# A hybrid encoder layer on one core: two chunk chains started together, and the second pair's transposes among the last chunks

## The chip, the cores and the metric

The kernel runs on 1 core of one Trainium2 chip. The metric is the device time of one execution in microseconds, as the median of several runs. The engines are TensorE (PE; its weight loads are PEld), VectorE (DVE), ScalarE (ACT) and GpSimd (POOL), and SyncE (SP), which issues most transfers.

## The reference

Two sequences (`x_prompt`, `x_sample`) of 1024 rows and 1024 columns go through the same layer. All numbers are float32.

```
h   = rmsnorm(x, g_mix) * (1 + sc1) + sh1
z   = h @ w_in                      # q_lat, kv_lat, k_pe, f_in
mix = concat(mla(q_lat, kv_lat, k_pe), fourier(f_in)) @ w_out
x   = x + ga1 * mix
h2  = rmsnorm(x, g_ffn) * (1 + sc2) + sh2
x   = x + ga2 * ((silu(h2 @ w_gate) * (h2 @ w_up)) @ w_down)
y   = rmsnorm(x, g_final)
```

The vectors `sh1`, `sc1`, `ga1`, `sh2`, `sc2`, `ga2` are slices of `silu(c) @ w_ada + b_ada`, one set for each sequence. Only `h` and `z` of the first rows, and the weights that are prepared for them, concern this change.

## The kernel before

A float32 product is made of three matmuls of two rounded parts each (`mm3`, lines 79 to 81): high by high, high by low, low by high. `split` (63, 64) makes the parts: a cast on ACT and a subtraction on DVE.

The first stage makes z and the Fourier input of all rows. Rows are taken in eight pairs of 128 (`pairs`; four for each sequence): the two halves u = 0, 1 of a pair are turned into their sum ("even") and difference ("odd"), and both are multiplied by the input weights: `z_mm` by `wz` (448 columns), `f_mm` by `wcs` (280 or 256 columns), in eight steps c of 128 channels each. Pairs 2 to 7 load x already transposed (`xt_load`), scale it by the row norms, which PE spreads with two transposes (`scale_t`, 450), and make even and odd on POOL (`evenodd`, 497).

Pairs 0 and 1 run while weights still arrive. Their x is loaded in rows, `norm` (425) takes squares on ACT (423), a root on POOL (`rstd`, 104 to 111), scales the rows (435, 436) and makes sum and difference (441, 150, 153); `flip` (464) transposes two channel blocks of both by PE (475), and ACT and DVE apply scale and shift and split the result (478 to 485).

The scale `s1` and shift `sh1` that `flip` needs come from the first 2048 columns of `w_ada`. They are made in four **chunks** g of 2 MB, each for two channel blocks: `cols_load` (248) fetches it, `cols_mm` (256) multiplies it by silu(c) into a row, `cols_vecs` copies the row to `modrow` on ACT (261), turns it with four small matmuls (264), and DVE writes `s1`, `sh1` (271 to 275). Then `flip(0, g)`, `z_part(g)` and `f_part(g)` (12 matmul rows each) follow for pair 0. Beside this run `prep` (392 to 402: the Fourier weights from `w_in`), `wz_split` (387), and `fold_out` (310, 311: `w_uv` of each of four heads multiplied into `w_out`, with a store to `wo_d`).

`first_pair` then evacuates pair 0 (`z_finish`, 529 to 537), transposes pair 1's rows (`flip(1, g)`), and transposes pair 0's latents (`latents`, 580). `pair(k)` does the rest, with `between` as a hook in the middle of z. The generator `extras`, advanced by `next(more)`, loads eight tiles of further `w_ada` columns (231) and multiplies them (241), one "conditioning group" of eight matmuls for each.

Order: each engine runs its own queue in order. `then` and `behind` (`tc.issue_after`) put a function behind the last matmul, cast or subtraction written; within these bounds the order on an engine is set when the program is built, and a tile's new owner waits for its last user. SP issues loads and stores in the order of its queue, so a load that waits for a tile holds all that is behind it. Tiles matter in three places: `xtile` (four of 4 KB), `wada_tile` (two slots of 8 KB) and the `wide` tiles `hh0`, `hh1`, `hl0`, `hl1`, used in turn for weights, chunks, output weights and later x. PSUM has eight banks.

## Time and profile before

| | us |
|---|---|
| times of three runs | 2021.83, 2017.2, 2017.96 (median 2017.96) |
| the profiled execution: time | 2021.76 |
| its span | 2020.0 |
| PE busy in the span | 1979.0 (98%) |
| DVE busy | 1389.5 (69%) |
| ACT busy | 897.1 (44%) |
| POOL busy | 844.1 (42%) |

The span is what the trace covers; all places below are in us from its start. "Busy" is the union of an engine's instructions; matmuls overlap, so a row's second number (its own duration) is more than the distance to the next row, and only distances between starts tell the rate. `[1.20 <-ACT eoh L481]` in a row is idle time before it and what ended it. An "x8" joins consecutive instructions. The granted clock is TensorE's, 1.00 at full speed.

### The profile page before, as it was taken

To read this page: it belongs to the slowest core of one execution; us is meant where nothing else is said; L and a number is where in the kernel's file an instruction comes from. 1 tells how busy PE (TensorE), PEld (TensorE's weight loads), DVE (VectorE), ACT (ScalarE), POOL (GpSimd) and SP (SyncE) were. 2 spreads that over 40 slices of the span, in tenths; PEclk is the share of its full clock that TensorE was granted. 3 is DMA by queue.
4 is the path that set the end of the run, shared out by engine and by line. 5 is a ranking of instruction groups with operands and counts; after the bars stand their busy time and mean duration, and the time that the engine had idled before them with its cause. 6 is when DMAs were issued, how large, how long until landed. Compare 5 with 4: busy or idle time off the path is not lost.

```text
span 2020.0 us, 27660 instructions
## 1 busy us (share of the span) xinstructions
PE 1979.0 (98%) x9554; PEld 1622.5 (80%) x9554; DVE 1389.5 (69%) x2083; ACT 897.1 (44%) x1750; POOL 844.1 (42%) x1000
## 2 busy tenths in 40 slices
PE   7899999999999999999999999999999999999998
PEld 5688778888888877888888878887888888888886
DVE  4467757766687778677777567788755655656794
ACT  4665535555565564333333356443333333335551
POOL 0364312111223237878879410344654454420152
PEclk8899999999999999999999999999999999999999
DMA  8886984445543575555545586665333233257762
GB/s 348 292 297 202 306 325 118 120 98 123 148 117 108 184 262 200 194 170 199 194 159 196 172 311 231 220 224 190 122 105 105 99 110 105 99 192 248 250 229 88
DMA packets 179593, 376.59 MB, mean 186 GB/s; under 512 B 18012, under 2 KB 57564, under 8 KB 175740
## 3 DMA queue, kind: packets, MB, share of 16 engines
q1 hardware_dynamic: 157052, 305.60, 45.2%
q0 software_dynamic: 21824, 68.17, 11.0%
q8 instruction: 75, 1.23, 0.2%
q10 hardware_dynamic: 576, 1.05, 0.1%
q14 instruction: 66, 0.54, 0.1%
HBM read 262.75 MB, written 120.39 MB: 190 GB/s over the span
## 4 chain that ended last, share of the span: by engine, by line
PE 54%; DVE 4%; issue 2%; DMA 1%; POOL 1%; ACT 0%; SPq 0%; DVEq 0%; POOLq 0%; ACTq 0%
PE bank L80 18%; PE bank L79 18%; PE bank L81 18%; DVE wl L64 2%; DMA draw<-s_d 1%; DVE val L153 0%; DVE val L1873 0%; DMA val<-x_d 0%; DVE H L64 0%; DVE val L1901 0%; DVE val L1792 0%; ACT wh L63 0%; POOL rs_y L107 0%; POOL val L153 0%; DVE val L150 0%
## 5 line engine op out<-in xcount | busy, mean ns | idle before, releaser
L79 PE MATMUL bank<-H,wh 128*128 128x512 f32 x1232 | 480.5, 390 | 3.5 <-DVE val L153 1.4
L80 PE MATMUL bank<-H,wh 128*128 128x512 f32 x1232 | 479.5, 389 | 0.3 <-DVE H L64 0.3
L81 PE MATMUL bank<-H,wl 128*128 128x512 f32 x1232 | 479.3, 389 | 0.2 <-DVE wl L64 0.2
L79 PEld LDWEIGHTS bank<-H,wh 128*128 128x128 f32 x1232 | 231.3, 188 | 55.2 <-DVE val L1775 3.2
L64 DVE TENSOR_TENSOR wl<-draw,wh 128x512 fp32r<-128x512 f32 x286 | 210.1, 773 | 93.9 <-ACT wh L63 93.3
L81 PEld LDWEIGHTS bank<-H,wl 128*128 128x128 f32 x1232 | 231.3, 188 | 48.8 <-DVE wl L64 0.5
L80 PEld LDWEIGHTS bank<-H,wh 128*128 128x128 f32 x1232 | 231.3, 188 | 48.0 <-DVE H L64 0.6
L153 DVE TENSOR_TENSOR val<-bank,val 128x512 f32<-128x512 f32 x200 | 136.6, 689 | 161.3 <-PE bank L81 160.4
L63 ACT CAST wh<-draw 128x512 fp32r<-128x512 f32 x286 | 164.9, 619 | 175.5 <-PE bank L80 145.3
L153 POOL TENSOR_TENSOR val<-val 128x512 f32<-128x512 f32 x58 | 82.1, 1417 | 347.2 <-DVE val L1873 163.8
L80 PE MATMUL bank<-wl,wh 128*128 128x512 f32 x572 | 223.5, 391 | 1.8 <-DVE wl L64 1.7
L79 PE MATMUL bank<-wh 128*128 128x512 f32 x572 | 222.8, 390 | 1.2 <-ACT wh L63 1.1
L81 PE MATMUL bank<-wh,wl 128*128 128x512 f32 x572 | 222.6, 389 | 0.0
L63 ACT CAST wh<-rgu 128x512 fp32r<-128x512 f32 x172 | 107.1, 623 | 258.6 <-PE bank L80 202.3
L63 ACT CAST wh<-val 128x512 fp32r<-128x512 f32 x133 | 82.3, 622 | 261.3 <-PE bank L80 242.4
L64 DVE TENSOR_TENSOR wl<-val,wh 128x512 fp32r<-128x512 f32 x133 | 129.7, 977 | 66.2 <-ACT wh L63 66.1
L64 DVE TENSOR_TENSOR wl<-rgu,wh 128x512 fp32r<-128x512 f32 x172 | 160.0, 930 | 1.6 <-ACT wh L63 1.6
L150 POOL TENSOR_TENSOR val<-rgu 128x512 f32<-128x512 f32 x80 | 108.1, 1351 | 79.0 <-DMA rgu<-in_wgu_dram 75.2
L80 PEld LDWEIGHTS bank<-wl,wh 128*128 128x128 f32 x572 | 107.4, 188 | 26.9 <-DVE wl L64 4.7
L79 PEld LDWEIGHTS bank<-wh 128*128 128x128 f32 x572 | 107.4, 188 | 24.5 <-ACT wh L63 2.0
L81 PEld LDWEIGHTS bank<-wh,wl 128*128 128x128 f32 x572 | 107.4, 188 | 21.8
L150 POOL TENSOR_TENSOR val<-val 128x512 f32<-128x512 f32 x89 | 119.1, 1356 | 1.3
(398 smaller groups left out, 3917.2 us busy)
## 6 DMA issues: line engine op xcount, KB each, us to landing
rgu<-in_wgu_dram SPq DMA_DIRECT2D x86, 512.0 KB, 3.9
draw<-s_d SPq DMA_DIRECT2D x143, 256.0 KB, 3.3
s_d<-val POOLq DMA_DIRECT2D x88, 256.0 KB, 3.0
draw<-t_d SPq DMA_DIRECT2D x88, 256.0 KB, 4.2
s_d<-val SPq DMA_DIRECT2D x66, 256.0 KB, 3.8
draw<-in_w_down_dram SPq DMA_DIRECT2D x55, 256.0 KB, 4.2
xt<-in_x_dram SPq DMA_DIRECT2D x16, 512.0 KB, 8.3
wada<-in_w_ada_dram SPq DMA_DIRECT2D x16, 512.0 KB, 6.4
```

The lines of the kernel that those rows point to most:

```text
L63: here["a"] = nc.scalar.copy(hi, src).ins
L64: here["v"] = (eng or nc.vector).tensor_tensor(out=lo, in0=src, in1=rd(hi), op=ALU.subtract).ins
L79: nc.tensor.matmul(out, lh, rh, start=first, stop=False, skip_group_check=cont)
L80: nc.tensor.matmul(out, lh, rl, start=False, stop=False, skip_group_check=cont)
L81: here["t"] = here["pe"] = nc.tensor.matmul(out, ll, rh, start=False, stop=last, skip_group_check=cont).ins
L150: return eng.tensor_tensor(out=out, in0=x, in1=y, op=ALU.subtract).ins
L153: eng.tensor_tensor(out=out, in0=x, in1=y, op=ALU.add)
```

## The change

- The transfers on SP get another order. Chunk 0 and the second pair of Fourier weights go ahead of `wz`; chunks 1 to 3 go ahead of the output weights (`wo_load`), and chunk 2 now lies in the `wada` slots, chunk 3 in `hl0` and `hh0`, output weights 0 in a `wada` slot. `x_load(1)` stands ahead of chunk 3; `xt_load(2)`, `x_load(2)` follow the output weights.
- `cols_mm(1)`, `cols_vecs(1)` and `flip(0, 1)` stand ahead of `z_part(0)`, and likewise each following chunk one step earlier, so that the chain of one chunk runs beside the products of the one before.
- `norm(1)` comes beside chunk 3 (its sum goes to the `lq` tile), `flip(1, 0)` to `flip(1, 3)` between `z_part` and `f_part` 2 and 3, the folded heads between them; `norm(2)` starts in `first_pair`.
- The heads are folded in place (`fold_head`) and stored together (`fold_store`).
- Pair 0's latents and two steps of `more` move from `first_pair` to the first hook in pair 1's z.
- The even rows of pairs 0 and 1 share a tile (`st1["even"]`), and the second half of the subtraction goes from POOL to DVE.

The core of the diff:

```diff
@@ -434,11 +434,11 @@
                 return
             nc.scalar.activation(xt[0], xt[0], AF.Copy, scale=r[:, 0:1])
             nc.vector.tensor_scalar(out=xt[1], in0=xt[1], scalar1=r[:, 1:2], scalar2=None, op0=ALU.mult)
-            xe = w.tile([P, D], F32, tag="eo", name="xe", bufs=1)
+            xe = lq[0].rearrange("p a b -> p (a b)") if k else w.tile([P, D], F32, tag="eo", name="xe", bufs=1)
             for g in range(2):
                 gs = slice(512 * g, 512 * g + 512)
                 add(xe[:, gs], xt[0][:, gs], xt[1][:, gs], nc.vector)
-                sub(xt[0][:, gs], xt[0][:, gs], xt[1][:, gs], nc.gpsimd if g else nc.vector)
+                sub(xt[0][:, gs], xt[0][:, gs], xt[1][:, gs], nc.vector)
             st1["rows", k] = xe, xt[0]
 
         def scale_t(k):
@@ -464,9 +464,10 @@
         def flip(k, g):
             s, j = pairs[k]
             if g == 0:
-                st1["hf", k] = w3.tile([P, NC, 2, P], F32, tag="hf", name="hf", bufs=1)
+                if k == 0:
+                    st1["even"] = w3.tile([P, 2, NC, P], F32, tag="hf", name="hf", bufs=1)
                 st1["eo", k] = eo_tiles(k)
-            hf = st1["hf", k]
+            hf = st1["even"][:, k]
             (eh, el), (oh, ol) = st1["eo", k]
             pt = bank().rearrange("p (c u t) -> p c u t", c=2, u=2)
             for c in range(2):
@@ -475,14 +476,14 @@
                     here["pe"] = nc.tensor.transpose(pt[:, c, u, :], st1["rows", k][u][:, cc * P : (cc + 1) * P], ident).ins
             for c in range(2):
                 cc = 2 * g + c
-                nc.scalar.activation(hf[:, cc, 0], pt[:, c, 0], AF.Identity, bias=dsh[:, cc : cc + 1], scale=s1[s][:, cc : cc + 1])
+                nc.scalar.activation(hf[:, cc], pt[:, c, 0], AF.Identity, bias=dsh[:, cc : cc + 1], scale=s1[s][:, cc : cc + 1])
             for c in range(2):
                 cc = 2 * g + c
                 here["o"] = nc.scalar.activation(oh[:, cc], pt[:, c, 1], AF.Copy, scale=s1[s][:, cc : cc + 1]).ins
                 nc.vector.scalar_tensor_tensor(out=ol[:, cc], in0=pt[:, c, 1], scalar=s1[s][:, cc : cc + 1],
                                                in1=rd(oh[:, cc]), op0=ALU.mult, op1=ALU.subtract)
             gs = slice(2 * g, 2 * g + 2)
-            split(eh[:, gs], el[:, gs], hf[:, gs, 0, :])
+            split(eh[:, gs], el[:, gs], hf[:, gs])
 
         def evenodd(k):
 
@@ -575,7 +576,7 @@
             ti = 4 * u + j
             sk = st1.pop(("sk", k, u))
             pl = bank()
-            with tc.issue_after(here["t"]) if k > 0 else ExitStack():
+            with tc.issue_after(here["t"]):
                 for c in range(4):
                     nc.tensor.transpose(pl[:, c * P : (c + 1) * P], sk[:, c * P : (c + 1) * P], ident)
             if k + 1 < nk:
@@ -666,96 +667,95 @@
                 for c in range(2 * g, 2 * g + 2):
                     f_mm(0, pc[i], i, c)
 
-        def fold_heads(h, wo, outs):
-            then(fold_out, h, wo, wuvT, outs)
+        def fold_head(h):
+            t = (wo0, wo1)[h // 2]
+            then(fold_out, h, t, wuvT, [t[:, h % 2, 512 * g : 512 * g + 512] for g in range(2)])
+
+        def fold_store():
+            for dst, t in folded:
+                nc.sync.dma_start(dst, t)
+            folded.clear()
 
         wf_pair(0, "hh0")
         fold_q(wukT)
-        prep(0)
+        ring = [xtile() for _ in range(2)]
         x_load(0)
+        wt.append([cols_load(0, i, wada_tile()) for i in range(2)])
+        prep(0, 1, 2, 3)
+        norm(0)
+        wf_pair(2, "hl0")
         wz0 = wz_load(0, wide("hh1", (P, 4 * 512)))
-        wt.append([cols_load(0, i, wada_tile()) for i in range(2)])
-        prep(1)
-        norm(0)
-        prep(2, 3)
-        wf_pair(2, "hl0")
-        wt.append([cols_load(1, 0, *(xtile().rearrange("p (c n) -> p c n", n=512) for _ in range(2))), cols_load(1, 1, wide("hh0"))])
-        wz1 = wz_load(4, wide("hl1", (P, 4 * 512)))
-        wt.append([cols_load(2, i, wide(f"h{'hl'[i]}{1 - i}")) for i in range(2)])
-        pz, pc = ([bank() for _ in range(2)] for _ in range(2))
-        then(cols_mm, 0, wt[0])
-        wz_split(0, wz0)
-        prep(4, 5)
-        then(cols_vecs, 0)
-        then(flip, 0, 0)
+        wt.append([cols_load(1, 0, *(t.rearrange("p (c n) -> p c n", n=512) for t in ring)), cols_load(1, 1, wide("hh0"))])
         wuvT = w.tile([P, HEADS, KVL], F32, tag="gah1", name="wuvT")
         nc.sync.dma_start(wuvT, a["wuvT"])
         wpe = lq[1][:, 0].rearrange("p (a b) -> p a b", a=2)
         nc.sync.dma_start(wpe, a["wpe"])
+        wz1 = wz_load(4, wide("hl1", (P, 4 * 512)))
+        wt.append([cols_load(2, i, wada_tile()) for i in range(2)])
+        pz, pc = ([bank() for _ in range(2)] for _ in range(2))
+        then(cols_mm, 0, wt[0])
+        prep(4, 5)
+        then(cols_vecs, 0)
+        then(flip, 0, 0)
+        wz_split(0, wz0)
         prep(6, 7)
+        then(cols_mm, 1, wt[1])
+        x_load(1)
+        wt.append([cols_load(3, i, wide(f"h{'lh'[i]}0")) for i in range(2)])
+        then(cols_vecs, 1)
+        then(flip, 0, 1)
         wz_split(2, wz0)
         then(z_part, 0)
-        then(cols_mm, 1, wt[1])
-        wo0 = wo_load(0, wide("hl1", (P, 2, D)))
-        wt.append([cols_load(3, i, wada_tile()) for i in range(2)])
-        x_load(1)
+        then(cols_mm, 2, wt[2])
+        wo0 = wo_load(0, wada_tile().rearrange("p a b -> p (a b)").rearrange("p (a b) -> p a b", a=2))
+        fold_pe(wpe)
         then(f_part, 0)
-        then(cols_vecs, 1)
-        then(flip, 0, 1)
-        for i in (4, 6):
-            wz_split(i, wz1)
+        then(cols_vecs, 2)
+        then(flip, 0, 2)
+        wz_split(4, wz1)
         then(z_part, 1)
-        then(cols_mm, 2, wt[2])
+        then(cols_mm, 3, wt[3])
         wo1 = wo_load(1, wide("hl0", (P, 2, D)))
+        wz_split(6, wz1)
+        norm(1)
+        then(f_part, 1)
+        then(cols_vecs, 3)
+        then(flip, 0, 3)
+        then(z_part, 2)
+        xt_load(2)
         nc.sync.dma_start(ropec, a["ropec"])
         nc.sync.dma_start(ropes, a["ropes"])
-        then(f_part, 1)
-        then(cols_vecs, 2)
-        then(flip, 0, 2)
-        fold_pe(wpe)
-        fold_heads(0, wo0, (w.tile([P, 512], F32, tag="gah0", name="so"), lq[0][:, 0]))
-        then(z_part, 2)
-        then(cols_mm, 3, wt[3])
+        x_load(2)
+        then(flip, 1, 0)
         then(f_part, 2)
-        then(cols_vecs, 3)
-        then(flip, 0, 3)
-        fold_heads(1, wo0, [lq[g][:, 1] for g in range(2)])
-        with behind(), tc.issue_after(here["o"]):
-            norm(1)
-        for dst, so in folded:
-            nc.sync.dma_start(dst, so)
-        folded.clear()
+        then(flip, 1, 1)
+        fold_head(0)
+        then(z_part, 3)
+        then(flip, 1, 2)
+        fold_head(1)
+        then(f_part, 3)
+        then(flip, 1, 3)
+        more = extras()
+        next(more)
         nc.sync.dma_start(wq_d, wq)
         nc.sync.dma_start(sc_d, scT)
         nc.sync.dma_start(cmask, a["cmask"])
-        x_load(2)
-        more = extras()
-        next(more)
-        then(z_part, 3)
-        then(f_part, 3)
+        x_load(3)
+        fold_store()
         for h in (2, 3):
-            fold_heads(h, wo1, [wo1[:, h % 2, 512 * g : 512 * g + 512] for g in range(2)])
+            fold_head(h)
         wf.clear()
         lq.clear()
 
         def first_pair():
             z = z_finish(0, pz)
             next(z)
-            for g in range(4):
-                flip(1, g)
+            norm(2)
             next(more, None)
             next(z, None)
             for i in range(2):
                 f_finish(0, i, pc[i])
-            for u in range(2):
-                latents(0, u)
-            next(more, None)
-            next(more, None)
-            xt_load(2)
-            x_load(3)
-            for dst, so in folded:
-                nc.sync.dma_start(dst, so)
-            norm(2)
+            fold_store()
 
         def late_latents(k):
             if k > 0:
@@ -784,6 +784,11 @@
                     prepare(k + 1)
                     if k < 2:
                         norm(k + 2)
+                if c == 1 and k == 1:
+                    for u in range(2):
+                        latents(0, u)
+                    next(more, None)
+                    next(more, None)
                 if c == 1:
                     flush()
                 else:
```

What the order on the engines becomes. First PE, at the first z of pair 0: L392 is `prep`, L256 `cols_mm`, L264 `cols_vecs`, L475/L476 the transposes of `flip`, L79 to L81 with `wz` the z product. Before:

```order
L392 MATMUL bank_353<-c2_136,wide_269 128x128 x4
L392 MATMUL bank_364<-c2_136,wide_269 128x128 x4
L79 MATMUL bank_284<-wz_h_130,eoh_333 128x448
L80 MATMUL bank_284<-wz_l_131,eoh_333 128x448
L79 MATMUL bank_285<-wz_h_130,eoh_335 128x448
```

and now:

```order
L392 MATMUL bank_353<-c2_136,wide_269 128x128 x4
L392 MATMUL bank_364<-c2_136,wide_269 128x128 x4
L256 MATMUL bank_375<-xt_194,scT_141 32x512 x2
L256 MATMUL bank_375<-xt_193,scT_141 32x512 x2
L256 MATMUL bank_375<-wide_276,scT_141 32x512 x4
L264 MATMUL bank_394<-wq_129,modrow_392 128x2 x4
L476 MATMUL bank_403<-ident_67,xe_264 128x128
L476 MATMUL bank_403<-ident_67,xt_195 128x128
L476 MATMUL bank_403<-ident_67,xe_264 128x128
L476 MATMUL bank_403<-ident_67,xt_195 128x128
L79 MATMUL bank_287<-wz_h_130,eoh_334 128x448
L80 MATMUL bank_287<-wz_l_131,eoh_334 128x448
```

Chunk 1's matmuls, small matmuls and transposes moved ahead of the first z matmul; the small matmuls read `modrow`, which ACT has to write first.

Next PE in pair 1's z, at the transposes of `scale_t` (L450); L241 is a conditioning group. Before:

```order
L450 MATMUL bank_849<-ident_67,rs_r_810 128x128 x2
L79 MATMUL bank_824<-wz_h_130,eoh_676 128x448
L80 MATMUL bank_824<-wz_l_131,eoh_676 128x448
L241 MATMUL bank_787<-wada_784,scT_141 32x512 x4
L81 MATMUL bank_824<-wz_h_130,eol_677 128x448
L79 MATMUL bank_824<-wz_h_130,eoh_676 128x448
```

and now:

```order
L450 MATMUL bank_846<-ident_67,rs_r_741 128x128 x2
L79 MATMUL bank_795<-wz_h_130,eoh_583 128x448
L80 MATMUL bank_795<-wz_l_131,eoh_583 128x448
L81 MATMUL bank_795<-wz_h_130,eol_584 128x448
L79 MATMUL bank_795<-wz_h_130,eoh_583 128x448
L80 MATMUL bank_795<-wz_l_131,eoh_583 128x448
```

The second conditioning group went from here to pair 2's z, 108 rows later. Groups two to five now stand in pair 2: between them 11 z rows, then the latents and 10 f rows, then 17 f rows.

Last ACT, at the end of pair 0: L311 is a folded half head, L529/L530 and L542 to L544 `z_finish` with its squares, L478/L479 and L481/L482 the casts of `flip`. Before (`flip` of pair 1 follows behind):

```order
L529 ACTIVATE lat_655<-bank_284 128x448
L423 ACTIVATE junk_584,ms_581<-xt_405 128x1024
L610 COPY zc0_108<-bank_286 128x280
L542 ACTIVATE junk_659,mz_653<-lat_654 128x256
L543 ACTIVATE junk_659,mz_653<-lat_654 128x128
L435 ACTIVATE xt_404<-xt_404,rs_r_589 128x1024
L311 ACTIVATE wide_469<-bank_641,pk_140 128x512
L311 ACTIVATE wide_469<-bank_644,pk_140 128x512
L311 ACTIVATE wide_469<-bank_647,pk_140 128x512
L542 ACTIVATE junk_662,mz_653<-lat_655 128x256
L311 ACTIVATE wide_469<-bank_650,pk_140 128x512
L543 ACTIVATE junk_662,mz_653<-lat_655 128x128
```

and now:

```order
L611 COPY zc0_108<-bank_289 128x280
L543 ACTIVATE junk_720,mz_711<-lat_713 128x256
L479 ACTIVATE hf_333<-bank_672,wq_129,s1_77 128x128 x2
L482 ACTIVATE eoh_583<-bank_672,s1_77 128x128
L63 CAST eoh_583<-hf_333 128x256
L311 ACTIVATE wide_502<-bank_699,pk_140 128x512
L482 ACTIVATE eoh_583<-bank_672,s1_77 128x128
L311 ACTIVATE wide_502<-bank_702,pk_140 128x512
L311 ACTIVATE wide_502<-bank_705,pk_140 128x512
L311 ACTIVATE wide_502<-bank_708,pk_140 128x512
L544 ACTIVATE junk_720,mz_711<-lat_713 128x128
L611 COPY zs0_110<-bank_290 128x256
```

The last square of pair 0 (L543, now L544) stood behind four folded half heads and ahead of pair 1's casts; now it stands behind the same four and also behind the casts of all four flips of pair 1.

## The prediction

> **What bounds the kernel now.** I read the profile from whole to part: first the stretches of 20 us, then who TensorE (PE) waited for, then the timelines of the engines in the first 100 us. The stretches (columns: PE, weight loads, DVE, ACT, POOL busy, granted clock, DMA share, GB/s):
>
> ```profile
> 40.00:60.00 20.00, 20.00 (x123) 13.87 (x116) 4.96 (x22) 11.13 (x28) 1.15 (x3) 1.00 0.94 370
> 60.00:80.00 20.00, 14.92 (x66) 9.24 (x64) 11.23 (x32) 14.72 (x39) 8.66 (x20) 0.83 0.55 178
> 80.00:100.00 20.00, 15.71 (x88) 13.04 (x87) 7.82 (x19) 10.37 (x28) 7.54 (x8) 0.83 1.04 390
> 100.00:120.00 20.00, 20.00 (x130) 15.92 (x129) 10.61 (x23) 13.46 (x34) 12.70 (x25) 1.00 0.68 244
> ```
>
> From 40 to 60 and from 100 on PE is busy throughout; the lack is between: 5.1 us idle in 60 to 80 and 4.3 in 80 to 100, at a clock of 0.83. That is the place of this change. Everything behind 100 us has the same work in the same order but for the conditioning matmuls and a few stores, so a gain here is carried to the end. The waits of PE in the first 110 us:
>
> ```profile
> PE bank L241 <- DMA wada<-in_w_ada_dram: 4.3, 1, 4.3
> PE bank L450 <- POOL rs_r L111: 1.8, 1, 1.8
> PE bank L580 <- DVE lat L556: 1.7, 1, 1.7
> PE bank L79 <- ACT eoh L481: 1.2, 1, 1.2
> PE bank L475 <- DVE xt L150: 1.1, 1, 1.1
> ```
>
> Together 10.1 us. A wait costs more than itself: the matmuls behind it run slowly. After the 1.2 us wait for `eoh`:
>
> ```profile
> 35.12 0.74 PE L79 MATMUL bank<-wz_h,eoh 128*128 128x448 f32 x1 [1.20 <-ACT eoh L481]
> 38.58 0.37 PE L79 MATMUL bank<-wz_h,eoh 128*128 128x448 f32 x1
> ```
>
> Between these starts lie nine matmuls in 3.46 us, 0.38 each, against 0.20 later: about 1.5 us lost behind a wait of 1.2.
>
> **What the pieces cost.** The last chunk's rows on PE show each piece by the start of the next:
>
> ```profile
> 48.34 1.92 PE L256 MATMUL bank<-wada,scT 128*32 128x512 f32 x16
> 50.19 0.40 PE L79 MATMUL bank<-wcs_h,eoh 128*128 128x280 f32 x1
> 51.78 0.95 PE L264 MATMUL bank<-wq,modrow 128*128 128x2 f32 x8
> 52.58 0.30 PE L475 MATMUL bank<-ident,xe 128*128 128x128 f32 x1
> 53.05 1.88 PE L310 MATMUL bank<-wide,wuvT 128*128 128x512 f32 x4
> 54.70 0.47 PE L79 MATMUL bank<-wz_h,eoh 128*128 128x448 f32 x1
> 57.30 0.29 PE L79 MATMUL bank<-wcs_h,eoh 128*128 128x280 f32 x1
> 58.78 3.60 PE L310 MATMUL bank<-wide,wuvT 128*128 128x512 f32 x8
> 68.42 2.14 PE L580 MATMUL bank<-ident,lat 128*128 128x128 f32 x8 [1.66 <-DVE lat L556]
> 70.50 1.94 PE L241 MATMUL bank<-wada,scT 128*32 128x512 f32 x8
> 72.36 0.58 PE L79 MATMUL bank<-wz_h,eoh 128*128 128x448 f32 x1
> 92.51 0.29 PE L79 MATMUL bank<-wcs_h,eoh 128*128 128x280 f32 x1
> 98.44 0.36 PE L79 MATMUL bank<-wz_h,eoh 128*128 128x448 f32 x1
> ```
>
> Chunk matmuls 1.85, `f_part` 1.6, `cols_vecs` 0.8, `flip` 0.47, one folded head 1.65, `z_part` 2.6. Heads 2 and 3 took 3.6. The latents' eight transposes took 2.08 (four transposes of a `flip` took 0.47, so 0.94 would do: half clock again), one conditioning matmul group (L241) 1.86, pair 1's f 5.93 and its z (48 rows at 0.205) 9.8.
>
> The point to which I compare is pair 2's first z matmul, 98.44. The order moves the second conditioning group (1.86 us of work) from ahead of this point to behind it, so the old mark to be beaten is 96.6.
>
> **Start: chunk 1's row ahead of the first z.** Rows:
>
> ```profile
> 18.18 1.94 PE L256 MATMUL bank<-wada,scT 128*32 128x512 f32 x8 [0.47 <-DMA wada<-in_wada_dram]
> 20.04 2.70 PE L392 MATMUL bank<-c,wide 128*128 128x128 f32 x16
> 24.89 0.81 ACT L478 ACTIVATE hf<-bank,wq,s 128x128 f32<-128x128 f32 x2
> 28.62 0.18 ACT L401 CAST wcs_h<-bank 128x24 fp32r<-128x24 f32 x1 [0.35 <-DVE wcs_l L397]
> 20.87 1.07 DVE L64 TENSOR_TENSOR wz_l<-wide,wz_h 128x896 fp32r<-128x896 f32 x1
> GB/s 77 371 417 432 432 429 404 402 415 424 414 382 50 6 316 435 416 410 357 333 244 326 320 403 117 6 0 118 275 334 414 393 397 418 356 401 404 30 0 141
> ```
>
> The last row holds 40 slices of 2.75 us. `wz0` (128 x 1792 floats, 0.92 MB) now stands behind chunk 0 and the second weight pair. At about 430 GB/s these land 2.1 us earlier: chunk 0's second half starts at 16.05 instead of 18.18, and with its 1.94 the weight pair's matmuls start at 18.0 instead of 20.04. So `hf(0,0)` on ACT goes from 24.89 to 22.9.
>
> Chunk 1 has the same 9.2 MB ahead of its end as before. The slices add up to this at 24.7 us, and half a chunk's matmuls (0.9) end at 25.7. Then PE stands before `cols_vecs` 1, which needs a copy of chunk 1's row (modrow) on ACT. Before, `z_part` 0 filled this time. ACT has, from `hf` to its last weight cast, 3.9 us of work in the old rows (24.89 to 28.8). New in this stretch are the two casts of `wz_h`, each with a DVE partner of 1.07 us, for which the small casts at the end wait: 2.1. So 22.9 + 3.9 + 2.1 = 28.9, and the copy of 0.6 makes 29.5: **`cols_vecs` 1 starts at V = 29.7**, after a wait of 4.0. No row shows this wait; its bounds are 0.8 (the copy alone: V = 26.5) and 5.3 (V = 31, if the alternating ACT and DVE casts hide nothing of one another). I take 4.0, since it is put together from durations of the same instructions. Half clock behind it is charged with the 1.5 above.
>
> **From V to the folds.** In PE's order, us behind V: `flip(0,1)` ends at 1.3; `z_part` 0 with 1.5 for the clock 5.4; chunk 2 7.2; `f_part` 0 8.8; `cols_vecs` 2 and `flip(0,2)` 10.1; `z_part` 1 12.7; chunk 3 14.5; `f_part` 1 16.1. The transfers are in time: chunk 2 ends 12.8 MB, by the slices 33.3 us, needed at V + 5.4 = 35.1; chunk 3 ends 15.9 MB, 41 us at 410 GB/s, needed at 42.4. Before, the slices of 50 and 6 GB/s show the queue standing still at 33 to 38, behind the output weights; these now stand behind.
>
> Then ACT again. `norm(1)` now runs here, and row 3's copy stands behind its last step L435:
>
> ```profile
> 53.29 0.81 ACT L478 ACTIVATE hf<-bank,wq,s 128x128 f32<-128x128 f32 x2 [2.38 <-PE bank L475]
> 57.40 1.09 ACT L423 ACTIVATE junk<-xt 128x1024 bf16<-128x1024 f32 x1
> 58.35 0.24 ACT L423 ACTIVATION_READ_ACCUMULATOR junk<-xt 128x1 f32 x1
> 60.85 1.15 ACT L435 ACTIVATE xt<-xt,rs_r 128x1024 f32<-128x1024 f32 x1 [1.29 <-POOL rs_r L111]
> ```
>
> `hf` follows the start of `cols_vecs` by 1.5 (51.78 to 53.29), so it is at V + 10.3. Then one flip's first three casts, 1.3, and one square with its read, 1.2, end at 12.8; from the end of the read to L435 passed 2.3 (58.59 to 60.85) by way of POOL, so L435 runs from 15.0 to 16.1, the copy to 16.6. `cols_vecs` 3 starts at 16.7, a wait of 0.6 (bounds 0 and 1.9). `flip(0,3)` ends at 18.0, `z_part` 2 at 20.6. This short wait, with the nearly empty `cols_vecs` and `flip` behind it, resembles the 1.2 us one, so I charge its 1.5 again: 22.1. The Trainium skill, "TensorE: Matmul & The Clock Gate", section "Why this matters for your kernels", says that only idle gaps above about 3 us send the clock to half; the row at 35.12 contradicts it with 1.2 us. By the page this 1.5 would be left out and the time be 2008.5.
>
> Next: `flip(1,0)`, `f_part` 2, `flip(1,1)`, head 0, `z_part` 3: 0.47 + 1.6 + 0.47 + 1.65 + 2.6 = 6.8, to 28.9. `flip(1,2)`, head 1, `f_part` 3, `flip(1,3)`, heads 2 and 3: 0.47 + 1.65 + 1.6 + 0.47 + 3.6 = 7.8, to 36.7. Here z of pair 1 starts, at once: the old wait for `xt` (1.1) and the first part of that for `lat` are gone, since transposes and latents now have work beside them.
>
> **The latents.** They stand behind eleven z matmuls (2.3), at V + 39.0, and need `z_finish` of pair 0. ACT's rows:
>
> ```profile
> 61.91 1.82 ACT L311 ACTIVATE wide<-bank,pk 128x512 f32<-128x512 f32 x3
> 64.78 0.21 ACT L543 ACTIVATION_READ_ACCUMULATOR junk<-lat 128x1 f32 x1
> 69.63 0.41 ACT L63 CAST eoh<-hf 128x256 fp32r<-128x256 f32 x1
> 71.12 0.44 ACT L63 CAST eoh<-hf 128x256 fp32r<-128x256 f32 x1
> ```
>
> A flip's casts take 1.5 on ACT when nothing delays them (69.63 to 71.12), a folded half head 0.6. ACT from `z_part` 3's end at 28.9: copy of `lat` 0.4, `flip(1,2)` and head 1 2.7, squares and a copy 1.5, `flip(1,3)` and heads 2 and 3 3.9, together 8.5, so 37.4. PE's last fold at 36.7 and its cast set the same time, 37.3. Last square 0.5: 37.9. Then as before from the square's read (ending 64.99) to the latents at 68.42: 3.4, to 41.3. So **the wait for `lat` stays, at 2.3** (bounds 0 and 4), with the slow transposes of the 2.08.
>
> From 41.3: latents 2.1, conditioning group 1.9, thirteen z matmuls 2.7, transposes of `rs_r` 0.3, 24 z matmuls 4.9, f 5.9: 59.1. With V = 29.7, 88.8 against 96.6: **7.8 us gained**. The 4.3 us wait for `w_ada` and the 1.8 for `rs_r` are gone in this: that load's matmuls now stand behind pair 1's f, and pair 2's squares come while heads are folded.
>
> **What is moved beside this.** *Loads.* `x_load(1)`, `xt_load(2)` and `x_load(2)` are issued earlier on SP, all ahead of the folds; the old row shows what that saves, DVE standing before `scale_t`'s product:
>
> ```profile
> 87.13 2.48 DVE L453 TENSOR_TENSOR xT<-xT,bank 128x512 f32<-128x512 f32 x4 [9.91 <-DMA xT<-in_xt_dram]
> ```
>
> I count nothing for it, since PE's wait for `w_ada` covered it; without the move it would be late next, at 84 or so. `wuvT` and `wpe` (0.5 MB) now go ahead of `wz1`, which costs chunk 2 the 1.2 us that are in its 12.8 MB. *Stores.* The folded heads are written in place and stored later: the tile of heads 0 and 1 is a `wada` slot, freed by its stores behind `x_load(3)`; the tile of heads 2 and 3 is freed by stores that SP issues behind pair 0's `ckv_d`, hence near V + 44, and `xt_load(3)` waits for them. It is needed in the middle of pair 2's z, V + 64, 20 us later; nothing up to 4 us if SP is held up. *Even and odd rows of pair 2.* From `scale_t` to pair 2's z there are 24 z rows and f, 10.8 us. Before, the same chain had its product at 87.13 and its z at 98.44, 11.3 us, without a listed wait: tight, counted as nothing, bounds 0 and 1. *The subtraction* of the second half goes from POOL to DVE: nothing, since other casts stand beside it; at most the 1.1 us that PE waited for `xt`.
>
> The profiled execution took 2021.76 (span 2020.0), the median is 2017.96; two of the four times lie near 2021.8. 2021.76 - 7.8 = 2014.0, and from the median **2010**. I take the latter, since the new time will be a median too.
>
> **Rivals.** *ACT is the bound in both places.* For: ACT was busy 14.7 us of the 20 in 60 to 80 already, and its pieces now fall into less time. If durations add without overlap, V is 31.0, the latents wait 4.0, `cols_vecs` 3 waits 1.9: 4.3 us more, a gain of 3.5: 2014.5. Against: back to back the rows overlap.
>
> *No wait remains.* V = 26.5, no wait at the other two places and no half clock behind them: 3.2 + 0.6 + 2.3 + 1.5 + 1.5 + 1.1, 10 more: 2000. Against: each of the three waits is a chain of rows that the order only moves.
>
> *The change only moves the wait for `w_ada`.* Four conditioning groups (two loads each) now stand close together in pair 2, and the load of the third needs the slot of the first:
>
> ```profile
> wada<-in_w_ada_dram SPq DMA_DIRECT2D x16, 512.0 KB, 6.4
> ```
>
> Eleven z rows, a group, the latents and ten f rows lie between, 2.3 + 1.9 + 2.1 + 1.3 = 7.6 us, against 6.4 from issue to landing: tight. Two waits of the old 4.3 give all back: about 2018. For: each load waits on SP behind others. Against: before, the fourth group was as near behind its slot's release, and the stretch 100 to 120 shows PE full.
>
> *Slower: chunk 3 is late.* Its two loads stand on SP behind `x_load(1)`, whose tiles are held by chunk 1 until 25.7. Each us of landing after 42.4 is lost; from 50.2 on the kernel is slower than before. With landing at 53.4 the time is 2021. For: chunk 3 was needed only at 48.34 before. Against: the queue moves 400 GB/s whenever it is fed.
>
> **Chances.** Forecast (2006 to 2013) 0.60, ACT 0.22, no wait 0.06, `w_ada` 0.06, slower 0.06. The range 2003.5 to 2017.5 leaves out "no wait", "slower" and half of `w_ada`, 0.15. Below 2011.9 (0.3%, what a measurement of this kernel can tell from no change) lie 0.52 of the forecast and "no wait", 0.58; slower by as much needs a landing after 56, 0.03; the rest is 0.39.
>
> **What would show it.** Right: `cols_vecs` 1 on PE near 29.7 after a wait for ACT's modrow; half clock in `z_part` 0; `cols_vecs` 3 waiting briefly behind L435; pair 1's z starting near 66; a wait of about 2 for `lat`; none for `w_ada` in pair 1; pair 2's z near 89. Wrong: chunk waits on DMA, clock 0.5 over more than 6 us, or new waits for `w_ada` between 90 and 130.

## The result

The changed kernel takes 2012.48 us in the median of 7 runs (2008.76 to 2015.05), beside 2018.45 for the kernel before (7 runs, 2017.2 to 2021.83). The ratio is 0.9967, 95% interval 0.9956 to 0.9979: 6.0 us less. In a second series the same two kernels gave 2012.01 and 2020.46, ratio 0.996 (0.9947 to 0.9972). Forecast was 2010. The profiled execution took 2011.69, its span is 2009.9, 10.1 less than before.

Places are again us from the start of the span. In the changed kernel the lines of the helpers stand one further down (latents 581, flips 476), those of stage 2 five (1168 for 1163).

First the stretches of 20 us, with the columns of before (PE, weight loads, DVE, ACT, POOL busy, granted clock, DMA share, GB/s):

```profile
20.00:40.00 20.00, 14.99 (x98) 10.95 (x97) 11.70 (x32) 12.40 (x31) 0.00 (x0) 0.83 1.02 421
40.00:60.00 20.00, 19.58 (x118) 15.08 (x118) 10.48 (x34) 12.70 (x32) 1.95 (x7) 1.00 0.89 329
60.00:80.00 20.00, 17.88 (x95) 13.83 (x94) 9.24 (x27) 17.51 (x44) 8.94 (x24) 1.00 0.75 258
80.00:100.00 20.00, 20.00 (x131) 16.88 (x129) 12.86 (x30) 14.00 (x34) 14.46 (x23) 1.00 0.84 270
220.00:240.00 20.00, 18.39 (x76) 11.32 (x80) 14.45 (x21) 7.65 (x13) 5.01 (x3) 0.91 0.98 362
```

The first and the last of these stretches before the change:

```profile
20.00:40.00 20.00, 18.22 (x120) 14.74 (x120) 10.35 (x31) 9.27 (x26) 0.00 (x0) 0.88 0.73 290
220.00:240.00 20.00, 19.30 (x109) 14.89 (x108) 18.01 (x33) 11.41 (x27) 4.07 (x2) 1.00 1.04 352
```

Between 60 and 100 PE now idles 2.1 instead of 9.4 us, and its clock is 1.00 instead of 0.83. The lack has moved to both ends: 20 to 40 (5.0 us idle instead of 1.8, clock 0.83 instead of 0.88) and 220 to 240 (1.6 instead of 0.7, 0.91 instead of 1.00). The waits of PE up to 110, the three longest besides the first load:

```profile
PE bank L264 <- ACT modrow L261: 4.2, 3, 3.3
PE bank L581 <- DVE lat L557: 2.1, 1, 2.1
PE bank L256 <- DMA wide<-in_wada_dram: 1.4, 1, 1.4
```

The waits for `w_ada`, `rs_r`, `eoh` and `xt` are gone, that for `lat` has stayed, that for `modrow` is new. PE's rows at the forecast's places, in order of time:

```profile
29.89 1.87 PE L264 MATMUL bank<-wq,modrow 128*128 128x2 f32 x8 [3.26 <-ACT modrow L261]
36.11 1.92 PE L256 MATMUL bank<-wada,scT 128*32 128x512 f32 x16
43.40 1.92 PE L256 MATMUL bank<-wide,scT 128*32 128x512 f32 x16
47.42 1.05 PE L264 MATMUL bank<-wq,modrow 128*128 128x2 f32 x8 [0.42 <-ACT modrow L261]
69.78 1.08 PE L581 MATMUL bank<-ident,lat 128*128 128x128 f32 x8 [2.12 <-DVE lat L557]
70.79 1.06 PE L241 MATMUL bank<-wada,scT 128*32 128x512 f32 x8
85.54 0.36 PE L79 MATMUL bank<-wz_h,eoh 128*128 128x448 f32 x1
```

`cols_vecs` 1 starts at 29.89 (forecast 29.7), chunks 2 and 3 start without a wait for their transfers, the latents wait 2.12 (2.3), and pair 2's z starts at 85.54 (88.8), beside 98.44 before. The rows of ACT behind the waits for `modrow`:

```profile
23.14 0.81 ACT L479 ACTIVATE hf<-bank,wq,s 128x128 f32<-128x128 f32 x2
28.84 0.18 ACT L401 CAST wcs_h<-bank 128x24 fp32r<-128x24 f32 x1 [0.96 <-DVE wcs_l L397]
29.17 0.18 ACT L401 CAST wcs_h<-bank 128x24 fp32r<-128x24 f32 x1
29.25 0.59 ACT L261 COPY modrow<-bank 128x512 f32<-128x512 f32 x1
45.74 1.15 ACT L435 ACTIVATE xt<-xt,rs_r 128x1024 f32<-128x1024 f32 x1 [2.00 <-POOL rs_r L111]
46.80 0.56 ACT L261 COPY modrow<-bank 128x512 f32<-128x512 f32 x1
```

Row 1's copy stands behind the last two weight casts, the first of which waited 0.96 us for DVE, and row 3's behind L435, as forecast.

**How far the lead is carried.** At pair 2's z it is 12.9; less the one conditioning group that now comes later (1.06), 11.8. The last of the eight latents groups starts at 203.26, before at 215.02: still 11.8. But the last conditioning matmul of stage 2 (line 1168) starts at 265.8, before (1163) at 274.5: 8.7. Between them 3.1 us went. The timeline of SP and PE at this place, first after the change and then before:

```profile
213.10 2.42 SPq L1154 DMA_DIRECT2D scT<-sc_d  x1
215.57 0.43 SPq L1156 DMA_DIRECT2D bT<-in_bT_dram  x1
216.05 0.43 SPq L1158 DMA_DIRECT2D gT<-in_gT_dram  x1
216.57 1.33 SPq L1173 DMA_DIRECT2D wada<-in_w_ada_dram  x3
...
221.61 1.04 PE L1168 MATMUL bank<-wada,scT 128*32 128x512 f32 x2 [2.36 <-DMA wada<-in_w_ada_dram]
```

```profile
226.43 0.86 SPq L1168 DMA_DIRECT2D wada<-in_w_ada_dram  x2
...
231.41 1.04 PE L1163 MATMUL bank<-wada,scT 128*32 128x512 f32 x2 [0.70 <-DMA wada<-in_w_ada_dram]
```

In both, the matmul follows 5.0 us behind the load's issue. The issue came 9.9 us earlier, PE 11.8 earlier, so PE waits 2.36 instead of 0.70. The half clock behind the wait (0.91 in 220 to 240, before 1.00) costs about 1.8 us by that share of 20 us; with the 1.7 more of waiting this makes 3.5, a little over the 3.1 that went.

### The profile page after: what moved, and what is told of

Its sections match the earlier page's. It is cut to its first block, busy times and chain, and to the rows that moved or that the text cites. A ratio compares the mean times of both kernels' runs of the same rounds, so it can differ in the third digit from the quotient of the medians.

```text
span 2009.9 us, 27661 instructions
## 1 busy us (share of the span) xinstructions
PE 1974.1 (98%) x9554; PEld 1623.2 (81%) x9554; DVE 1393.2 (69%) x2085; ACT 897.5 (45%) x1750; POOL 840.5 (42%) x998
## 4 chain that ended last, share of the span: by engine, by line
PE 57%; DVE 4%; issue 1%; POOL 1%; DMA 1%; ACT 0%; DVEq 0%; POOLq 0%; ACTq 0%
PE bank L80 19%; PE bank L79 19%; PE bank L81 19%; DVE wl L64 1%; DVE val L1878 1%; DVE val L153 1%; DMA draw<-s_d 0%; DVE val L1906 0%; DMA val<-x_d 0%; DVE H L64 0%; POOL rs_y L107 0%; ACT wh L63 0%; POOL val L153 0%; DVE val L150 0%; POOL out_dram L1912 0%
## 5 line engine op out<-in xcount | busy, mean ns | idle before, releaser
L79 PE MATMUL bank<-H,wh 128*128 128x512 f32 x1232 | 480.6, 390 | 3.3 <-DVE val L153 1.4
L81 PE MATMUL bank<-H,wl 128*128 128x512 f32 x1232 | 479.3, 389 | 0.2 <-DVE wl L64 0.2
L79 PEld LDWEIGHTS bank<-H,wh 128*128 128x128 f32 x1232 | 231.2, 188 | 55.0 <-DVE val L1780 2.9
L81 PEld LDWEIGHTS bank<-H,wl 128*128 128x128 f32 x1232 | 231.2, 188 | 48.4 <-DVE wl L64 0.5
L79 PE MATMUL bank<-wh 128*128 128x512 f32 x572 | 222.7, 389 | 0.2 <-ACT wh L63 0.2
L81 PE MATMUL bank<-wh,wl 128*128 128x512 f32 x572 | 222.6, 389 | 0.0
L79 PEld LDWEIGHTS bank<-wh 128*128 128x128 f32 x572 | 107.4, 188 | 23.0 <-ACT wh L63 0.6
L81 PEld LDWEIGHTS bank<-wh,wl 128*128 128x128 f32 x572 | 107.4, 188 | 22.1
```

Source lines behind the costliest of these rows:

```text
L79: nc.tensor.matmul(out, lh, rh, start=first, stop=False, skip_group_check=cont)
L81: here["t"] = here["pe"] = nc.tensor.matmul(out, ll, rh, start=False, stop=last, skip_group_check=cont).ins
```

## The experiments

The changed kernel is called "after" here. Each edit is made to it unless said otherwise. "z 2" is the start of pair 2's z, "lat 8" that of the last latents group, "c 8" that of the last conditioning matmul of stage 2, all on PE in one profile. The interval is that of the ratio to the kernel before, in runs on the same chip.

| kernel | z 2 | lat 8 | c 8 | median us (runs) | ratio, interval |
|---|---|---|---|---|---|
| before | 98.44 | 215.02 | 274.5 | 2018.45 (7) | 1 |
| before_again | 98.19 | 214.76 | 274.1 | 2017.65 (1) | |
| after | 85.54 | 203.26 | 265.8 | 2012.48 (7) | 0.9967, 0.9956 to 0.9979 |
| after_again | 85.30 | 203.02 | 265.8 | 2012.01 (5) | 0.996, 0.9947 to 0.9972 |
| one_chain | 89.75 | 209.46 | 268.0 | 2011.45 (5) | 0.9957, 0.9943 to 0.9971 |
| latents_back | 90.77 | 207.34 | 266.2 | 2012.7 (5) | 0.9962, 0.995 to 0.9975 |
| chunk3_behind | 90.08 | 207.94 | 269.8 | 2016.23 (11) | 0.9987, 0.9978 to 0.9996 |
| flips_back | 84.92 | 202.67 | 264.0 | 2008.88 (5) | 0.9944, 0.9931 to 0.9956 |
| prep_late | 88.35 | 206.07 | 267.3 | 2010.9 (5) | 0.9959, 0.9946 to 0.9971 |
| latents_later | 88.53 | 206.25 | 267.1 | 2012.15 (5) | 0.9966, 0.9954 to 0.9979 |
| mod2_late | 87.11 | 204.83 | 268.4 | 2010.61 (5) | 0.996, 0.9948 to 0.9973 |
| wm_first | 88.32 | 206.04 | 269.4 | 2010.78 (5) | 0.9965, 0.9952 to 0.9978 |
| flips_wm | 85.52 | 203.27 | 265.9 | 2008.68 (5) | 0.9945, 0.9931 to 0.996 |
| flips_wada | 84.57 | 202.33 | 263.0 | 2008.51 (5) | 0.9939, 0.9926 to 0.9953 |

**The two kernels again.** No edit.

> The kernel before the change, with a second profile. Theory A (the difference between its median and its profiled 2021.8 does not arise in the first 100 us): pair 2's first z again within 1 us of 98.4, the waits for w_ada, rs_r, lat, eoh and xt as before, and what is shorter lies behind 280. Theory B: a half clock or a wait of the first 100 us comes and goes, pair 2's z off by more than 1 us.

> The changed kernel as it is, once more, with a second profile. Theory A (the lead is made in stage 1 and is steady): pair 2's first z matmul within 1 us of 85.5, waits of about 3.3 for modrow, 2.1 for lat and 2.4 for stage 2's w_ada again, time 2010 to 2014. Theory B (the lead differs from execution to execution with the granted clock): pair 2's z off by more than 1 us, or the same mark with the time off by 2 us or more and the difference in stretches of lower clock behind 100 us.

Theory A by the marks of both: "z 2", "lat 8" and "c 8" lie within 0.4 us of the first profiles. A half clock did come and go, though: behind the wait for `lat` before_again is at full clock (1.00 in 60 to 80, before 0.83). PE then waits longer for `rs_r` (3.1 instead of 1.8), and the load of `w_ada` ends its next wait within 0.3 us of the same place. The span of before_again is 2015.9, 4.1 shorter, of which 3.7 lie behind "c 8" (1741.8 against 1745.5 us of the same work). Between these two executions most of the spread is made there and not at the change. In the seven runs of the changed kernel a lower mean granted clock goes with a longer time (2008.76 at 0.998, 2013.64 and 2013.83 at 0.994). In the 41 runs of the kernel before that stand beside the experiments it hardly does: 16 at 0.994 took 2019.7 on average, five at 0.996 2020.2.

The marks vary as well. mod2_late and wm_first below have the same instructions in stage 1 as after, and "z 2" at 87.11 and 88.32. In wm_first chunk 0 began 2.5 us later (16.17 against 13.66). In mod2_late the same wait for `lat` ended at the same place as in after, but half clock followed it:

```profile
69.78 1.75 PE L581 MATMUL bank<-ident,lat 128*128 128x128 f32 x8 [2.10 <-DVE lat L557]
71.46 1.94 PE L241 MATMUL bank<-wada,scT 128*32 128x512 f32 x8
```

From pair 1's z to pair 2's passed 20.7 us in after, after_again, prep_late and wm_first, and 22.2 to 22.3 in mod2_late, one_chain and chunk3_behind; the wait for `lat` was 2.1 in all seven. So 1.6 us of "z 2" can come and go with the execution. A difference of under 3 us in "z 2" is therefore read only with the wait that makes it, and the 10.1 between two profiles says less than the medians' 6.0 to 8.5 and the 8.7 at "c 8".

**Part by part: one chain at a time.** `cols_mm`, `cols_vecs` and `flip` of chunks 1 to 3 each go behind the preceding `z_part`, the new order of the loads stays:

```
+then(z_part, 0)
 then(cols_mm, 1, wt[1])
+then(f_part, 0)
 then(cols_vecs, 1)
 then(flip, 0, 1)
-then(z_part, 0)
...
```

> One chunk chain at a time as before the change (row 1 behind z_part 0, row 2 behind z_part 1, row 3 behind z_part 2), with the changed kernel's loads and with pair 1's flips still among the last chunks. Theory A (two chains at once gain): the wait of 3.3 for modrow at cols_vecs 1 goes, but PE waits between every flip and the z_part right behind it for the casts on ACT, 1 to 2 us three times, with half clock: 1 to 5 us longer than the changed kernel. Theory B (the second chain costs as much as it saves, its price being the modrow wait with its half clock, 4.8): the same or up to 3 us shorter.

The waits for casts came much as theory A has them; PE's waits of this kernel up to 100:

```profile
PE bank L79 <- ACT eoh L482: 2.4, 2, 1.2
PE bank L581 <- DVE lat L557: 2.1, 1, 2.1
PE bank L79 <- ACT wz_h L63: 1.6, 1, 1.6
```

Pair 1's z starts at 67.48 instead of 64.85, 2.6 late. "z 2" is 4.2 late; the other 1.6 are the half clock behind the wait for `lat`, which came in this execution. By the time it is theory B: the total is the same as that of after. Undone alone, the two chains are worth 2.6 us in stage 1 and nothing that the totals show.

**Part by part: the latents.**

```
 first_pair: f_finish(0, i, pc[i])
+    latents(0, 0), latents(0, 1), next(more), next(more)
 between:
-    if c == 1 and k == 1: latents(0, u); next(more); next(more)
```

> Pair 0's latents and the two steps of the side work behind them go back ahead of pair 1's z, all else as in the changed kernel. Theory A (the eleven z rows hide part of the way to lat): the wait for lat grows from 2.1 by the 2.3 us of those rows to 4.4, and half clock comes back behind it (about 1.0 in the transposes, 0.9 in the conditioning group): 2 to 4.5 us longer. Theory B (lat is late only because the rows stand ahead on ACT and DVE): wait unchanged, time within 1 us.

The wait grew as theory A has it, to the tenth, and the half clock came back:

```profile
69.98 1.91 PE L581 MATMUL bank<-ident,lat 128*128 128x128 f32 x8 [4.35 <-DVE lat L557]
```

"z 2" is 5.2 late, 4.2 without the group that stands ahead of it here. The total, by theory A 2 to 4.5 us longer, is again that of after (+0.7, within both intervals). Its stage 2 shows where the delay goes: PE waits 0.6 for the same load, not 2.4, at a clock of 1.00:

```profile
200.00:220.00 20.00, 20.00 (x164) 19.82 (x163) 16.23 (x38) 12.68 (x35) 9.69 (x15) 1.00 0.81 243
220.00:240.00 20.00, 19.40 (x85) 11.85 (x83) 17.23 (x25) 10.89 (x19) 4.22 (x3) 1.00 1.00 365
```

From "lat 8" to "c 8" it takes 58.9 us, after takes 62.5. Of 4.1 us at "lat 8", 0.4 are left at "c 8".

**Part by part: the loads' order.**

```
 then(cols_mm, 1, wt[1])
 x_load(1)
-wt.append([cols_load(3, i, ...) for i in range(2)])
...
 wo0 = wo_load(0, ...)
+wt.append([cols_load(3, i, ...) for i in range(2)])
```

> Chunk 3's two loads go behind the first output weights in SP's queue, hence behind PE's release of chunk 2's tile at 38. Theory A (the loads' order is what lets the second chain run): chunk 3 (2.1 MB behind 1 MB) lands near 46 instead of before 43.4, PE waits 2 to 3 us for it with half clock behind, pair 1's z 3 to 5 us later than 64.9; at the end 0 to 1 us of it is left if the start of stage 2 evens it out, all of it if not. Theory B: folds and transposes fill the time, pair 1's z within 1 us.

PE's waits of this kernel up to 100, the first row:

```profile
PE bank L256 <- DMA wide<-in_wada_dram: 5.2, 3, 2.2
```

Pair 1's z starts at 67.80, 2.9 late. "z 2" is 4.5 late, 1.6 of it by the half clock behind the wait for `lat`. Theory A, and this one is not evened out: 2016.23, 4 us above after, as "c 8" is 4.0 late, for waits on chunk transfers in that tile that were 3.8 us longer (1.4 in after). In its stage 2 PE waits 2.0 us for a weight cast ahead of line 1168, and "lat 8" to "c 8" takes 61.9: with nearly the "lat 8" of latents_back, stage 2 started the slow way. Its eleven runs spread the most here, from 2011.21 to 2021.16, so the size of these 4 us is the least certain in the table.

**Part by part: the flips.**

```
-then(flip, 1, 0) ... then(flip, 1, 3)      # among z_part, f_part, fold_head
 first_pair:
     next(z)
+    for g in range(4): flip(1, g)
```

> Pair 1's four flips go back from among the last chunks to behind pair 0's z, all else as in the changed kernel. Theory A (they are worth what they hide): the transposes' own work is the same 1.9 us, but PE again waits for the first casts of pair 1 (1.2 for eoh before the change) with half clock behind (1.5): 2 to 4 us longer than the changed kernel, and the wait for lat gets shorter or goes, since the flips stand ahead of it. Theory B (the loads' order and the moved latents make the gain, the flips none): within 1 us of the changed kernel.

Neither theory: the kernel is 3.1 us **shorter** than after_again in the same series, and the slowest of its five runs (2009.68) is below the fastest there (2010.22). PE's rows:

```profile
66.82 0.47 PE L79 MATMUL bank<-wz_h,eoh 128*128 128x448 f32 x1 [1.02 <-ACT eoh L63]
68.20 1.03 PE L581 MATMUL bank<-ident,lat 128*128 128x128 f32 x8
69.16 1.06 PE L241 MATMUL bank<-wada,scT 128*32 128x512 f32 x8
```

The wait for `eoh` is back with 1.02, but the one for `lat` (2.12) is gone. The flips fill time on PE, and their casts no longer stand on ACT ahead of pair 0's evacuation; its last square starts 5.7 us earlier, first in after, then here:

```profile
66.17 0.40 ACT L544 ACTIVATE junk<-lat 128x128 bf16<-128x128 f32 x1
60.45 0.30 ACT L544 ACTIVATE junk<-lat 128x128 bf16<-128x128 f32 x1
```

The wait for `xt` doesn't come back. "z 2" is 0.6 earlier, "c 8" 1.8. What makes up the rest of the 3.1 the profiles don't show.

**The wait for `modrow`.**

```
-prep(6, 7)
 then(cols_mm, 1, wt[1])
...
 then(flip, 0, 1)
+prep(6, 7)
```

> Weight preparation 6 and 7 goes from ahead of chunk 1 to behind flip(0,1), so that ACT's copy of row 1 no longer stands behind its six casts. Theory A: cols_vecs 1 starts at 27.2 instead of 29.9, the preparation's 2.3 us of PE work fill the time in which z_part 0 would wait for the casts, no half clock: z_part 0 starts 1 to 2 us earlier and 1.5 are saved in it; pair 1's z 2 to 3.5 us earlier. The total moves by less than 1 us all the same if the start of stage 2 takes the lead back; by 2 to 3.5 if it does not. Theory B: chunks 2 and 3 are not there yet, PE waits on their transfers instead, pair 1's z within 1 us of 64.9.

Missed by both theories: the wait fell to 0.70, but `cols_vecs` 1 starts at 29.67 all the same, and the preparation, at half clock, now takes 3.3 us behind it:

```profile
29.67 1.87 PE L264 MATMUL bank<-wq,modrow 128*128 128x2 f32 x8 [0.70 <-ACT modrow L261]
32.29 3.62 PE L392 MATMUL bank<-c,wide 128*128 128x128 f32 x16
```

PE came to that place at half clock already, behind a wait of 2.19 for the transfer of chunk 1. Pair 1's z is 2.8 late, "z 2" too; 1.6 of it were there at chunk 0 (15.24 against 13.66). The total is not worse than after (2010.9).

**The wait for `lat`.**

```
-if c == 1 and k == 1:
+if c == NC - 1 and k == 1:
     for u in range(2): latents(0, u)
```

> Pair 0's latents and the two steps behind them stand behind 23 z rows of pair 1 instead of 11. Theory A: the twelve more rows (2.5 us with the transposes of rs_r) cover the wait of 2.1: it goes, pair 2's z starts 2 us earlier, and the total is shorter by that or, if the start of stage 2 takes it back, by less than 0.5. Theory B: the conditioning groups behind stand closer and wait for their loads, pair 2's z within 0.7 of 85.5.

Missed: the wait for `lat` went, but PE came to the transposes of `rs_r` earlier and waited there, longer, and the half clock made the eight transposes and the group twice as long:

```profile
72.53 0.69 PE L450 MATMUL bank<-ident,rs_r 128*128 128x128 f32 x2 [3.18 <-POOL rs_r L111]
73.01 1.92 PE L581 MATMUL bank<-ident,lat 128*128 128x128 f32 x8
74.86 1.94 PE L241 MATMUL bank<-wada,scT 128*32 128x512 f32 x8
```

In after the wait for `lat` covers the old one for `rs_r`: the last step of `rs_r` starts on POOL at 73.24, and PE comes to the transposes at 74.52, hence without the 2.12 at 72.4. "z 2" is 3.0 late, the total that of after.

**The start of stage 2.** Three kernels. The first holds the conditioning groups in program order and one step later:

```
-if t > 1: mod2(t - 2)
+if t > 2: mod2(t - 3)
+    with tc.issue_after(here["t"]): nc.tensor.matmul(chunks["ps"]...)
```

> Only stage 2 is changed: its first conditioning group waits in program order for the matmuls ahead of it and each group stands one output step later, so that PE comes to the first 1 MB load at least 5 us later. Theory A (the start of stage 2 is bound by SP's queue: that load is issued at 216.6 whatever lead stage 1 has, and takes back 2.4 us by the wait and 1.5 by the half clock of 220 to 240): both go, 3 to 4 us shorter than the changed kernel, 2008 to 2009. Theory B (the queue's lateness only moves to the next transfers, the stores and the weights behind them): within 1 us of it.

The second also moves the loads `for c in range(3): mod2_load(c)` and `wq_l` behind `prep_wm(0, [1])`; the third adds the flips as in flips_back:

> The later conditioning groups of mod2_late, and in SP's queue the loads of the second half's output weights go ahead of the second and third 1 MB load and of wq. In mod2_late PE waited 1.3, 0.9 and 1.5 for casts of these weights, behind 3.8 MB in the queue. Theory A (the queue's order at the start of stage 2 takes the lead back): these waits go too, 230 to 240 is at full clock, 2 to 4 us shorter than mod2_late, hence 2007 to 2009 beside the changed kernel's 2012. Theory B (the bytes themselves, not their order): the waits show at the 1 MB loads again, within 1 us of mod2_late's 2010.6.

> wm_first with pair 1's flips back behind pair 0's z. Theory A (the two add up): flips_back was 3.1 us shorter than the changed kernel, of which about 1.3 by less half clock in stage 2's start that wm_first removes as well; so 1 to 2 us shorter than wm_first. Theory B (both only shorten the same wait): within 0.7 us of wm_first.

PE's waits from 200 to 300 in mod2_late, then in wm_first:

```profile
PE bank L1128 <- DVE wn L1100: 1.5, 1, 1.5
PE bank L79 <- ACT wm L63: 1.3, 1, 1.3
PE bank L80 <- DVE wm L64: 0.9, 1, 0.9
```

```profile
PE bank L79 <- ACT ea L1132: 2.6, 1, 2.6
PE bank L79 <- DVE nyl L64: 1.3, 1, 1.3
```

Theory B in both: the wait for the 1 MB load goes, and first the output weights behind it in the queue, then ACT's evacuation of the output steps take its place, 3.7 and 3.9 us in all. The totals stay at 2010.6 and 2010.8, with the ratios of after. flips_wm is 2.1 shorter than wm_first and equal to flips_back: only the flips count.

The last one is flips_back with the first 1 MB load ahead of `scT`, `bT`, `gT` in SP's queue:

```
+mod2_load(0)
 nc.sync.dma_start(scT, sc_d)
...
```

> flips_back with one change at the start of stage 2: the first 1 MB load of w_ada goes ahead of the three small loads (scT, bT, gT, 3.5 us of issue on SP in the changed kernel: 213.1 to 216.6) in SP's queue, the order of PE as in flips_back. Theory A (the issue on SP makes that load late): it is issued 2 to 3.5 us earlier, the wait of 1.5 for it goes, 1 to 2 us shorter than flips_back's 2008.9. Theory B (another chain of that place, the store and reload of lat or the evacuations by ACT and DVE, ends at the same time): the wait reappears before other matmuls, within 0.7 us of it.

The load was issued at 212.96 instead of 216.19, and PE then waited 1.0 for `scT` and 1.5 for `nyl`, before 1.5 for the load and 1.5 for `nyl`. 2008.51 beside 2008.88: theory B, the same within the interval. The three kernels with the flips back are the fastest measured here, 2008.5 to 2008.9, with ratios from 0.9939 to 0.9945.

## Why the prediction was right, and where not

**Right by mechanism.** The new wait at `cols_vecs` 1 (4.0 forecast, 3.26 measured, start off by 0.2), the brief one at `cols_vecs` 3 behind L435 (0.6; 0.42), the lasting one for `lat` (2.3; 2.12), chunks 2 and 3 in time, no wait for `w_ada` or `rs_r` in pair 1. Undoing a part made stage 1 later for the chains and the loads (2.6 and 2.9 at pair 1's z) and for the latents (4.2 at "z 2", with its half clock).

**Sizes off in the sum.** From V to pair 2's z 59.1 were forecast, 55.65 measured. Most of these 3.4 us are half clock that did not come. The 1.5 charged to `z_part` 2 did not, since row 47.42 and what follows are at full clock; here the Trainium skill, "TensorE: Matmul & The Clock Gate", section "Why this matters for your kernels", by which a gap of 0.42 us does nothing, was right and the analogy to the 1.2 us wait was not. The latents' transposes took 1.0 instead of 2.1 and the group behind them 1.0 instead of 1.9, both priced by rows of before that ran at half clock. That these two ran at full clock is luck of the execution: with the same wait, half clock followed in three of the seven kernels above, and before_again ran the same rows at full clock. So neither the charge nor its absence was to be had from the length of the wait. The other terms nearly cancel: the half clock behind V cost 0.8 more than charged (chunk 2 at V + 6.2 instead of 5.4), the part from `z_part` 2's end to pair 1's z took 13.6 instead of 14.6.

The group that moves behind this place was subtracted with the same 1.86 and is worth 1.06: 0.8 more. So the lead there was 11.8 instead of 7.8 (9.1 in the execution of wm_first).

**The step that failed.** "Everything behind 100 us has the same work in the same order but for the conditioning matmuls and a few stores, so a gain here is carried to the end." The work is the same, but what PE waits for there is not PE's own order: SP issues stage 2's first loads behind pair 7's stores, 9.9 us earlier where PE was 11.8 earlier. Of 11.8 us 8.7 are left at 266. That SP's queue alone sets this place is not shown: in flips_wada the load was issued 3.2 us earlier, and the total stayed. The rival of the `w_ada` wait that comes back looked for it in pair 2; it stood in stage 2, at another load of the same matrix. The lead too small by 4.0 and the 3.1 given back nearly cancel; that 2010 lies near 2012 is luck in this respect, and not a sum that was right.

**A part that was taken as a gain and is none.** The forecast let the wait for `xt` and the first part of that for `lat` go because "transposes and latents now have work beside them". Going back with the flips alone makes the kernel 3.1 us faster. The profiles show the wait for `lat` go with them, as their casts leave ACT, and 1.8 us of the gain at "c 8".

**Open.** one_chain, latents_back, latents_later and prep_late differ from after by 2.8 to 6.2 us at "lat 8" and by 1.6 at most in the median. Stage 2 absorbs this (58.5 to 62.5 us from "lat 8" to "c 8" for the same work), and three edits there only changed the name of the wait; which chain sets its end is not settled. Nor do the parts add up: undone alone, chunk 3's place among the loads is worth 4 us, the chains and the latents nothing that the totals show, the flips less than none, and the change as a whole 6.0 to 8.5. The other moves of loads and the smaller parts (the heads folded in place, `norm` 1 and 2 earlier, the subtraction on DVE) were not undone by themselves, and no two parts together.

## What to carry to other kernels

A lead won early is worth what is left of it at the next place where another engine or queue sets the time: read the issue of the loads there too, and carry the lead through it, before adding it to the end. A wait removed from a queue that runs through several engines returns at the next instruction of the same chain (`lat` to `rs_r`, the load to the weights to the evacuation). And undo each part of a composite change alone: here one of four costs more than it brings, two leave the total as it is, and the place of one load holds most of what is found. A price read from a row at half clock belongs to that execution; look at the same row in a second profile before adding it up.

## What the runs showed that was not expected

Half clock comes in pieces of about 3.4 us. In stretches of 20 us the granted clock was mostly 1.00, 0.91, 0.83, 0.74 or 0.66, that is 0, 3.6, 6.8, 10.4 or 13.6 us at half; other values, such as the 0.88 of before, fit a piece cut by the stretch's edge. Around `cols_vecs` 1, two kernels with the same work there, in stretches of 4 us (PE busy, clock, DMA share, GB/s), after and mod2_late:

```profile
28.00:32.00 4.00, 2.11 (x10) 0.50 1.01 425
32.00:36.00 4.00, 4.00 (x16) 0.65 1.01 419
```

```profile
24.00:28.00 4.00, 2.26 (x12) 0.70 1.03 417
28.00:32.00 4.00, 2.95 (x13) 0.50 1.01 421
32.00:36.00 4.00, 4.00 (x12) 0.52 1.02 424
```

Half clock lasted about 6.8 and 10.2 us. The Trainium skill's page "TensorE: Matmul & The Clock Gate", section "What's actually happening", has the clock follow a free-running window of 3.4 us, and these lengths agree with that. So a wait's own length says little. PE waited 3.26 us at this place in after and 1.38 in mod2_late, and chunk 2 started at 36.11 and 36.12. And behind the wait of 2.1 for `lat`, at 69.78 in both, after ran at full clock and mod2_late at half.
